# GpSimd in written order, the turning tables in two pieces, a tile's matrices in three

## The chip, the cores and the metric

The kernel runs on one core of a Trainium2 chip. The metric is device time in microseconds (us) of one execution, as the median of several runs. The engines are called by their names in the profile: PE is TensorE, DVE VectorE, ACT ScalarE, POOL GpSimd, SP SyncE (which here only issues DMAs).

## What is computed

One inference step of a decoder trunk: one S5 state-space layer and then one stick-breaking attention layer, over a prompt of 1024 tokens and eight samples of eight new tokens, with a model width of 1024. All of the change lies in the S5 layer:

```python
h = _rms_norm(x, g_pre)
uz = h @ w_in                                  # u and z, 1024 wide each
u, z = uz[..., :SSM_WIDTH], uz[..., SSM_WIDTH:]
...
lam_re, lam_im = mag * cos(dt * a_im), mag * sin(dt * a_im)
bu = w * (b @ u)                               # per group of 16 channels, 64 complex states
h[t] = lam * h[t - 1] + bu[t]                  # complex, over time
y = c_re @ h_re - c_im @ h_im + d_skip * u
...
y = gelu(y); y = y * sigmoid(y @ w_glu + b_glu); y = y * silu(z)
x = x + _rms_norm(y @ w_out, g_post)
```

(The middle lines are shortened from the reference's `_s5_scan`.) The attention layer behind it is the same before and after.

## The kernel before, in words

The time axis is cut in 128 chunks of L = 8 steps, and the eight samples are eight more columns, so that a row of a group is W = 136 columns wide. The 64 groups of 16 channels are worked through as eight tiles `ft` of eight groups; a tile's groups are done in three units of 3, 3 and 2 groups (`ACH`), j = 0, 1, 2. Beside the S5 work TensorE computes u and z themselves, x times w_in, as a stream of chunks called `fills` (`gemm`, L268): a chunk is 24 matmuls (three per 128 rows of x, since values are split in a high and a low part), and three chunks make 128 columns of u or z. A weight tile is split by `weights` (L217) and `split_w` (L138): a copy on ScalarE, and a subtraction on VectorE, or on GpSimd where z is odd.

For a tile `matrices(ft)` (L323) makes what the recurrence needs:

- On VectorE `wb`, and `ep` out of it by two products (`ep`, `tm`) and a subtraction, 1024 wide; eight transposes of `ep` on TensorE (L347), four at a time into one PSUM bank of the pool `m`, which has one buffer; each four are evicted by ScalarE to `et` (L348). VectorE also forms `fk` with `tn` (L351 to 353).
- After a `yield`, eight small matmuls K (L361) into the same bank, four evictions to `kp` (L369), `dk` on GpSimd and its addition on VectorE (L372), and eight DMAs that spread `kp` into `tg`.
- The turning tables: cosine and sine by products of short ones, two halves of three operations each into `cs` with the scratch tile `m`, on GpSimd (VectorE for tile 0), and four DMAs `cf<-cs` (L392) that copy them to all partitions. `cs` and `m` have one buffer, `cf` two.
- Eight DMAs `ug` that load the tile's u in another layout.

`states(ft, j)` (L402) is a unit: S matmuls (L409) into `psb`; two ScalarE copies to `tb` (L416, L417); VectorE multiplies `psb` by the cosine (`psb<-psb,cf`), GpSimd `tb` by the sine (`tb<-tb,cf`), VectorE adds (`psb<-psb,tb`), two or three scans (L424); and the same turning back: two copies to `ts` (L429, L430), `ts<-ts,cf` on GpSimd, `psb<-psb,cf` and the sum `hs` (L434) on VectorE. `outputs` (L438) follows two units later (`ULAG`): the O matmuls (L451, L452), the gelu to `gt` and the stores to `y_d`. All of the helper's `tensor_tensor` carry the line L207.

`manual_schedule` for PE keeps TensorE in the order of the text. The other engines' orders are set by a scheduler that plans by priorities, `OFA` being that of `states`, `outputs` and `matrices`. The main loop (L463 to L484) gives one unit per turn: `states`, a chunk, `outputs`, and in units 1 and 2 the next step of `matrices(ft + 1)`; in the first three tiles one more chunk. Behind the loop y is read back and split into `yh` and `yl` (L496 to L500), while the remaining chunks of z run, and the gate's GEMM (`whi_g`) follows.

Of the kernel before, what the change touches and what calls it, by code (L numbers as in the profile page):

```python
# [10 lines left out]
F32 = mybir.dt.float32  # L11
# [4 lines left out]
ALU = mybir.AluOpType  # L16
# [9 lines left out]
NC = SEQ // L  # L26
# [7 lines left out]
KT = 8  # L34
# [23 lines left out]
K_UBC, K_UBS, K_UAC, K_UAS, K_U = 0, 16, 32, 40, 48  # L58


def bc(ap, axis, n):
    shape = list(ap.shape)
    a = ap.unsqueeze(axis)
    shape.insert(axis, n)
    return a.to_broadcast(shape)
# [6 lines left out]
def rstd(nc, pool, ss, out, n, mul, tag, eng=None):  # L72

    E = eng or nc.vector
    v = pool.tile([128, n], F32, name=f"v_{tag}", tag="rs_v")
# [62 lines left out]
def split_w(nc, pool, raw, tag, shape, eng=None, bufs=2):  # L138

    hi = pool.tile(shape, F32R, name=f"whi_{tag}", tag="whi", bufs=bufs)  # L140
    lo = pool.tile(shape, F32R, name=f"wlo_{tag}", tag="wlo", bufs=bufs)
    nc.scalar.activation(hi, raw, AF.Copy)
    (eng or nc.vector).tensor_tensor(lo, raw, hi, op=ALU.subtract)
    return hi, lo
# [58 lines left out]
def s5_layer(tc, nc, io, wp, bank, cst, gains, ident, sgn, zs_d, u_d, y_d, s2):  # L203
    V, Q = nc.vector, nc.gpsimd

    def tt(eng, o, a, b, op):
        eng.tensor_tensor(o, a, b, op=op)  # L207

    with ExitStack() as sx:
        rows = sx.enter_context(tc.tile_pool(name="a_row", bufs=2, side="right"))  # L210
        big = sx.enter_context(tc.tile_pool(name="a_x", bufs=1, side="right"))
        st = sx.enter_context(ExitStack())
# [4 lines left out]
        def weights(which, ft):  # L217

            with tc.high_priority(2 * OFA):
                wraw = wp.tile([128, KT, 128], F32, name=f"wraw_{which}{ft}", tag="wraw", bufs=1)  # L220

                (nc.scalar if which == "u" else nc.sync).dma_start(wraw, io["a_win"][ft + (KT if which == "z" else 0)])
                return split_w(nc, wp, wraw, f"{which}{ft}", [128, KT, 128], Q if which == "z" and ft % 2 else V)


        gpre = start.tile([128, D], F32, name="gpre")
# [4 lines left out]
        for t in (8, 0, 1, 2, 3, 4, 5, 6, 7):  # L231
# [14 lines left out]
            for i in range(2):  # L246
# [6 lines left out]
                for c, (t0, m) in enumerate(ACH):  # L253
                    if t < 8:
                        if not t0 <= t < t0 + m:
                            continue
                        src, oh, ol = p3, xh[c][:, ks, t - t0, 0:NC], xl[c][:, ks, t - t0, 0:NC]
                        nc.scalar.activation(oh, src, AF.Copy)
                        tt(V, ol, src, oh, ALU.subtract)
                    else:  # L260
                        p4 = p3.rearrange("p a (s t) -> p a t s", t=TS)
                        src, oh, ol = p4[:, :, t0 : t0 + m], xh[c][:, ks, :, NC:W], xl[c][:, ks, :, NC:W]
                        nc.scalar.activation(oh, src, AF.Copy)
                        tt(V, ol, src, oh, ALU.subtract)
            if t == 0:
                w_first = weights("u", 0)
# [19 lines left out]
        def fill(n):  # L286
            for _ in range(n):
                next(fills, None)
# [7 lines left out]
        uu = par.tile([128, G // 2, K_U], F32, name="uu")  # L296
# [10 lines left out]
        tp = st.enter_context(tc.tile_pool(name="a_t", bufs=1, reuse_waits="tile"))  # L307
# [12 lines left out]
        sst = par.tile([128, G, NS], F32, name="sst")  # L320
        made, rows_in, rows_out, started = {}, {}, {}, {}

        def matrices(ft):  # L323

            gs = slice(ft * 8, ft * 8 + 8)
            pk = pk_all[:, gs, :]
            sb = tp.tile([128, 4, 8, GC], F32, name=f"sb{ft}", tag="sb", bufs=2)
            nc.scalar.dma_start(sb, io["s5_bc"][ft, :, 0:4])
            wb = tp.tile([128, 4, 8, GC], F32, name=f"wb{ft}", tag="wb")
            tt(V, wb[:, 0:2], sb[:, 0:2], bc(bc(wri[:, 0, gs], 2, GC), 1, 2), ALU.mult)  # L330
            tt(V, wb[:, 2:4], sb[:, 0:2][:, ::-1], bc(wri[:, 1:3, gs], 3, GC), ALU.mult)
            tt(V, wb[:, 0:2], wb[:, 0:2], wb[:, 2:4], ALU.add)
            V.tensor_scalar(sb[:, 2:4], sb[:, 2:4], sgn, None, op0=ALU.mult)

            ep = tp.tile([128, 8, L, GC], F32, name=f"ep{ft}", tag="ep")
            tm = tp.tile([128, 8, L, GC], F32, name=f"tm{ft}", tag="tm")
            lrv = pk[:, :, K_LR : K_LR + 8][:, :, ::-1]
            liv = pk[:, :, K_LI : K_LI + 8][:, :, ::-1]
            tt(V, ep, bc(lrv, 3, GC), bc(wb[:, 0], 2, L), ALU.mult)
            tt(V, tm, bc(liv, 3, GC), bc(wb[:, 1], 2, L), ALU.mult)  # L340
            tt(V, ep, ep, tm, ALU.subtract)
            et = tp.tile([128, 8, 128], F32, name=f"et{ft}", tag="et", bufs=2)
            for i in range(2):
                ps = bank("m")
                for j in range(4):
                    g = 4 * i + j
                    nc.tensor.transpose(ps[:, j * 128 : (j + 1) * 128], ep[:, g].rearrange("p a b -> p (a b)"), ident)  # L347
                nc.scalar.activation(et[:, 4 * i : 4 * i + 4, :], ps.rearrange("p (a b) -> p a b", a=4), AF.Copy)  # L348
            fk = tp.tile([128, 8, L + 1, GC], F32, name=f"fk{ft}", tag="fk", bufs=2)
            tm2 = tp.tile([128, 8, L + 1, GC], F32, name=f"tn{ft}", tag="tm")  # L350
            tt(V, fk, bc(pk[:, :, K_LR : K_LR + 9], 3, GC), bc(sb[:, 2], 2, L + 1), ALU.mult)  # L351
            tt(V, tm2, bc(pk[:, :, K_LI : K_LI + 9], 3, GC), bc(sb[:, 3], 2, L + 1), ALU.mult)
            tt(V, fk, fk, tm2, ALU.subtract)
            tg = tgs[ft % 2]
            yield
            kp = tp.tile([16, 8, 128], F32, name=f"kp{ft}", tag="kp")
            ps = bank("m")
            for i in range(2):
                for j in range(4):
                    g = 4 * i + j  # L360
                    nc.tensor.matmul(  # L361
                        ps[32 * j : 32 * j + 16, i * 128 : (i + 1) * 128],
                        wb[:, 0, g, :],
                        fk[:, g, 0:L, :].rearrange("p a b -> p (a b)"),
                        start=True,
                        stop=True,
                    )
            for j in range(4):
                nc.scalar.activation(kp[:, j::4, :], ps[32 * j : 32 * j + 16, 0:256].rearrange("p (a b) -> p a b", a=2), AF.Copy)  # L369
            dk = tp.tile([16, 8, GC], F32, name=f"dk{ft}", tag="dk")  # L370
            tt(Q, dk, bc(ident[:16, 0:16], 1, 8), bc(dcol[:, gs], 2, GC), ALU.mult)
            tt(V, kp[:, :, 0:GC], kp[:, :, 0:GC], dk, ALU.add)  # L372
            for t in range(L):
                nc.sync.dma_start(tg[t * GC : (t + 1) * GC, :, GC * t : 128], kp[:, :, 0 : 128 - GC * t])
            ph = uu[:, ft * 4 : ft * 4 + 4, :]
            cs = tp.tile([128, 2, 4, 8, 16], F32, name=f"cs{ft}", tag="cs")
            m = tp.tile([128, 4, 8, 16], F32, name=f"m{ft}", tag="m")
            uac, uas = (bc(ph[:, :, b : b + 8], 3, 16) for b in (K_UAC, K_UAS))
            ubc, ubs = (bc(ph[:, :, b : b + 16], 2, 8) for b in (K_UBC, K_UBS))
            E = Q if ft else V  # L380
            tt(E, cs[:, 0], uac, ubc, ALU.mult)
            tt(E, m, uas, ubs, ALU.mult)
            tt(E, cs[:, 0], cs[:, 0], m, ALU.subtract)
            tt(E, cs[:, 1], uas, ubc, ALU.mult)
            tt(E, m, uac, ubs, ALU.mult)
            tt(E, cs[:, 1], cs[:, 1], m, ALU.add)
            cof = tp.tile([128, 2, 8, NC], F32, name=f"cf{ft}", tag="cf", bufs=2)
            for i in range(2):
                src = cs[64 * i : 64 * i + 64].rearrange("p e g a b -> p e (g a b)")
                for h in range(2):  # L390
                    dst = cof[64 * h : 64 * h + 64, :, 4 * i : 4 * i + 4, :].rearrange("p e g c -> p e (g c)")
                    nc.sync.dma_start(dst, src)  # L392
            made[ft] = pk, et, fk, tg, cof[:, 0], cof[:, 1]

            ug = work.tile([128, 8, W], F32, name=f"ug{ft}", tag="ug")
            usrc = u_d[ft].rearrange("(g c) (t n) -> t c g n", c=GC, t=L)
            for t in range(L):
                nc.sync.dma_start(ug[t * GC : (t + 1) * GC], usrc[t])
            rows_in[ft] = ug
            yield  # L400
# [58 lines left out]
        def ahead(gen):  # L459
            with tc.high_priority(OFA):  # L460
                next(gen)

        first = matrices(0)  # L463
        fill(7)
        ahead(first)
        fill(1)
        ahead(first)
        nxt = None
        for n in range(3 * KT + ULAG):
            ft, j = divmod(n, 3)  # L470
            if n < 3 * KT:
                with tc.high_priority(OFA):
                    states(ft, j)
            if j == 1 and ft + 1 < KT:
                nxt = matrices(ft + 1)
            fill(1)
            if n >= ULAG:
                with tc.high_priority(OFA):
                    outputs(*divmod(n - ULAG, 3))
            if nxt and j:  # L480
                if j == 2 and ft < 3:
                    fill(1)
                ahead(nxt)
                nxt = nxt if j == 1 else None  # L484
# [958 lines left out]
```

## Time and profile before

| | |
|---|---|
| median of 3 runs | 1510.89 us (1508.28 to 1511.17) |
| profiled execution | 1508.97 us, its span 1507.2 us |
| mean granted clock of TensorE in the span | 0.982 |
| busy in the span: PE, DVE, ACT, POOL | 1417.8, 925.2, 716.4, 491.0 us |
| S5 layer | about the first 345 us of the span |

Times in the rows are in us from the start of the span, durations marked as means in groups are ns. A timeline row is: start, duration, engine, line, operation, what is written and read, the shape, and in brackets the engine's idle time before it and what ended it. A wait of several causes is named by the one that came last.

### The profile page before, as it was taken

How to read it: one execution, taken by the hardware profiler on the slowest of the kernel's cores; microseconds unless marked ns; L12 is line 12 of the kernel's file. 1: busy time of each engine (PE TensorE's matmuls, PEld its weight loads, DVE VectorE, ACT ScalarE, POOL GpSimd, SP SyncE). 2: the span in 40 equal slices, each digit the busy share in tenths (PEclk: the TensorE clock that was granted, in tenths of full speed). 3: DMA queues.
4: the chain of work that ended last, by engine and by line, in shares of the span. 5: the costliest groups of instructions: out<-in, count | busy, mean ns of one | idle time of the engine just before them, and what ended most of it. 6: DMA issues, size and time to landing. Idle time of an engine off the chain costs nothing.

```text
span 1507.2 us, 26829 instructions
## 1 busy us (share of the span) xinstructions
PE 1417.8 (94%) x9648; PEld 1150.1 (76%) x9648; DVE 925.2 (61%) x1507; ACT 716.4 (48%) x1424; POOL 491.0 (33%) x473
## 2 busy tenths in 40 slices
PE   4979878899999989999999999999998999998997
PEld 4979877899977879999988877666565665564766
DVE  6977887746754541010122149997888888789545
ACT  5324444544434533232333346675665657576321
POOL 6555656323421123222211012433323233334300
PEclk9998999999999999999999999999999999999999
DMA  5444555473223353232288764979877786754026
GB/s 196 114 139 115 151 146 137 129 252 135 71 92 120 112 203 116 84 114 87 87 311 295 257 233 159 352 268 332 294 277 273 263 288 231 260 201 140 11 80 214
DMA packets 129670, 276.41 MB, mean 183 GB/s; under 512 B 21633, under 2 KB 66562, under 8 KB 129538
## 3 DMA queue, kind: packets, MB, share of 16 engines
q1 hardware_dynamic: 127234, 268.41, 53.1%
q10 hardware_dynamic: 2304, 6.29, 1.3%
q8 instruction: 76, 1.25, 0.3%
q14 instruction: 56, 0.46, 0.1%
HBM read 224.55 MB, written 39.35 MB: 175 GB/s over the span
## 4 chain that ended last, share of the span: by engine, by line
PE 73%; DVE 6%; DMA 4%; issue 2%; POOL 2%; ACT 2%; SPq 1%; DVEq 0%; POOLq 0%; ACTq 0%
PE psmm L149 6%; PE psmm L151 6%; PE psmm L150 6%; PE psqk L150 6%; PE psqk L149 6%; PE psqk L151 6%; PE psa L992 5%; PE psb L1225 5%; PE psa L1033 4%; PE psb L1207 4%; PE psqk L1182 3%; PE psqk L1183 2%; PE psa L149 2%; PE psa L151 2%; PE psa L150 2%
## 5 line engine op out<-in xcount | busy, mean ns | idle before, releaser
L1163 POOL TENSOR_TENSOR ql<-q,qh 128x256 fp32r<-128x256 f32 x64 | 64.7, 1011 | 284.7 <-ACT qh L1162 240.1
L1184 ACT ACTIVATE F<-psqk,bp 128x384 f32<-128x384 f32 (+2 forms) x192 | 111.2, 579 | 63.6 <-PE psqk L1183 48.8
L1189 DVE TENSOR_TENSOR_SCAN F<-F,maskb 128x256 f32<-128x256 f32 (+3 forms) x128 | 130.8, 1027 | 16.0 <-ACT F L1184 15.5
L1192 POOL TENSOR_TENSOR S<-S,F 128x255 f32<-128x255 f32 (+3 forms) x64 | 100.5, 1571 | 115.3 <-DVE F L1191 28.5
L1185 ACT ACTIVATE S<-psqk,bp 128x384 f32<-128x384 f32 (+2 forms) x192 | 111.3, 582 | 22.5 <-PE psb L1207 22.5
L1207 PE MATMUL psb<-cst,S 128*128 128x128 f32 x576 | 96.8, 285 | 4.9 <-DVE og L1229 3.8
L1207 PEld LDWEIGHTS psb<-cst,S 128*128 128x128 f32 x576 | 67.1, 143 | 35.6 <-issue 20.5
L1191 DVE TENSOR_TENSOR_SCAN F<-F 128x384 f32<-128x384 f32 (+1 forms) x64 | 78.6, 1228 | 20.4 <-ACT F L1184 19.8
L1225 PE MATMUL psb<-at,vr 128*64 128x256 f32 (+1 forms) x640 | 90.0, 369 | 0.7 <-DVE at L1211 0.7
L992 PE MATMUL psa<-vp,sat 128*32 128x256 f32 x1024 | 86.0, 388 | 0.0
L1182 PE MATMUL psqk<-ks,qh 128*128 128x384 f32 (+2 forms) x192 | 77.6, 404 | 7.1 <-DVE ks L1147 5.4
L1033 PE MATMUL psa<-kp,qbd 128*32 128x256 f32 x1024 | 75.5, 389 | 0.4 <-PE psb L1207 0.4
L1225 PEld LDWEIGHTS psb<-at,vr 128*64 128x64 f32 x640 | 46.7, 137 | 36.1 <-issue 10.5
L1211 DVE TENSOR_TENSOR at<-psb,maskb 128x384 f32<-128x384 f32 (+3 forms) x128 | 60.2, 478 | 20.7 <-PE psb L1207 20.2
L149 PE MATMUL psmm<-x,whi_g 128*128 128x408 f32 (+1 forms) x192 | 66.6, 347 | 1.1 <-DVE gt L782 1.1
L149 PE MATMUL psmm<-xh,whi_u 128*128 128x408 f32 (+1 forms) x192 | 66.6, 347 | 0.2 <-ACT zt L277 0.2
L149 PE MATMUL psmm<-xh,whi_z 128*128 128x408 f32 (+1 forms) x192 | 66.7, 347 | 0.0
L986 DVE TENSOR_TENSOR_SCAN sF<-sF 128x513 f32<-128x513 f32 x32 | 44.4, 1388 | 36.1 <-ACT sF L983 35.8
L1182 PEld LDWEIGHTS psqk<-ks,qh 128*128 128x128 f32 x192 | 37.2, 194 | 38.1 <-ACT S L1185 13.0
L150 PE MATMUL psmm<-xl,whi_u 128*128 128x408 f32 (+1 forms) x192 | 65.4, 341 | 0.1
L1183 PE MATMUL psqk<-ks,ql 128*128 128x384 f32 (+2 forms) x192 | 65.5, 343 | 0.0
L150 PE MATMUL psmm<-x,whi_g 128*128 128x408 f32 (+1 forms) x192 | 65.1, 339 | 0.0
(452 smaller groups left out, 4224.4 us busy)
## 6 DMA issues: line engine op xcount, KB each, us to landing
kp<-cache_kT SPq DMA_DIRECT2D x128, 512.0 KB, 6.0
vp<-cache_v SPq DMA_DIRECT2D x128, 512.0 KB, 5.7
cf<-cs SPq DMA_DIRECT2D x32, 256.0 KB, 4.2
q<-q_d SPq DMA_DIRECT2D x128, 64.0 KB, 4.6
u_d<-ut SPq DMA_DIRECT2D x8, 544.0 KB, 2.9
ug<-u_d SPq DMA_DIRECT2D x64, 68.0 KB, 2.7
zs_d<-zt SPq DMA_DIRECT2D x8, 544.0 KB, 4.4
y_d<-gt SPq DMA_DIRECT2D x64, 68.0 KB, 2.3
```

What stands on the lines that cost most here:

```text
L149: nc.tensor.matmul(ps, sh, mh, start=(k == 0), stop=False)
L150: nc.tensor.matmul(ps, sh, ml, start=False, stop=False)
L151: nc.tensor.matmul(ps, sl, mh, start=False, stop=(k == n - 1))
L992: self.nc.tensor.matmul(po[32 * r : 32 * r + 32, 0:256], a[:, 32 * r : 32 * r + 32], rhs[:, r * 256 : (r + 1) * 256], start=start, stop=stop)
L1033: nc.tensor.matmul(ps[32 * r : 32 * r + 32, half * 256 : half * 256 + 256], self.qbd[:, 2 * r + e, s, :], kt[:, :, 2 * r + e, :], start=(e ...
L1182: nc.tensor.matmul(ps[:, :m], qh[:, w], ks[:, c0 : c0 + m], start=True, stop=False)
L1184: nc.scalar.activation(F[:, c0 : c0 + m], ps[:, :m], AF.Sigmoid, bias=bp[:, 1, h : h + 1], scale=-0.125)
L1185: nc.scalar.activation(S[:, c0 : c0 + m], ps[:, :m], AF.Sigmoid, bias=bp[:, 0, h : h + 1], scale=0.125)
L1189: V.tensor_tensor_scan(fr, fr, self.maskb[:, 512 - m : 512][:, ::-1], 1.0, ALU.mult, ALU.max)
L1192: (Q if i % 2 else V).tensor_tensor(S[:, 0 : n - 1], S[:, 0 : n - 1], F[:, 1:n], op=ALU.mult)
L1207: nc.tensor.transpose(ps[:, j * 128 : (j + 1) * 128], S[:, (j0 + j) * 128 : (j0 + j + 1) * 128], self.ident)
L1225: nc.tensor.matmul(po[hs, o:256], self.vr[pi][:, j, hs], ats[hh][j // 4][:, j % 4, o:256], start=(j == 0), stop=(j == nj - 1))
```

## The change

It has four parts. The subtraction of every z split runs on VectorE. `manual_schedule` holds GpSimd too, from the start of the loop's set-up: its instructions stand in the order of the text. The turning tables leave `matrices` for a generator `tables(ft)` with two steps, which the loop calls for the tile ahead, in units 0 and 1, right behind `states`; the four DMAs come with the second step. `matrices` yields once more, between its first and its second four transposes, so that it has three pieces, taken in unit 1, in unit 2 behind `states`, and at the end of unit 2. At the start one chunk more stands ahead of tile 0's first unit, six and three single ones, in place of seven and one.

```diff
-                return split_w(nc, wp, wraw, f"{which}{ft}", [128, KT, 128], Q if which == "z" and ft % 2 else V)
+                return split_w(nc, wp, wraw, f"{which}{ft}", [128, KT, 128])
...
+        st.enter_context(tc.manual_schedule(engines={mybir.EngineType.PE, mybir.EngineType.Pool}))
+        turns = {}
+        def tables(ft):
...
+            E = Q if ft else V
+            tt(E, cs[:, 0], uac, ubc, ALU.mult)
+            tt(E, m, uas, ubs, ALU.mult)
+            tt(E, cs[:, 0], cs[:, 0], m, ALU.subtract)
+            yield
+            cof = tp.tile([128, 2, 8, NC], F32, name=f"cf{ft}", tag="cf", bufs=2)
+            tt(E, cs[:, 1], uas, ubc, ALU.mult)
+            tt(E, m, uac, ubs, ALU.mult)
+            tt(E, cs[:, 1], cs[:, 1], m, ALU.add)
...
+                    nc.sync.dma_start(dst, src)
+            turns[ft] = cof
+            yield
...
             for i in range(2):
+                if i:
+                    yield
                 ps = bank("m")
...
-        first = matrices(0)
-        fill(7)
-        ahead(first)
-        fill(1)
-        ahead(first)
+        nxt = tables(0)
+        ahead(nxt)
+        ahead(nxt)
+        first = matrices(0)
+        fill(6)
+        for _ in range(3):
+            fill(1)
+            ahead(first)
         nxt = None
         for n in range(3 * KT + ULAG):
             ft, j = divmod(n, 3)
+            if j == 1 and ft + 1 < KT:
+                nxt = matrices(ft + 1)
             if n < 3 * KT:
                 with tc.high_priority(OFA):
                     states(ft, j)
-            if j == 1 and ft + 1 < KT:
-                nxt = matrices(ft + 1)
+            if j == 0 and ft + 1 < KT:
+                turn = tables(ft + 1)
+            if j < 2 and ft + 1 < KT:
+                ahead(turn)
+            if nxt and j == 2:
+                ahead(nxt)
             fill(1)
```

How this moves the instructions is seen at three places. The first is GpSimd in tile 1. `tb` and `ts` are the turnings of the units (0, 3, 6 is the unit's first group), `cs` and `m` the tables, `dk` the small product of `matrices`. Before:

```order
L207 TENSOR_TENSOR tb_0_1377<-tb_0_1377,cf_1359 128x384
L207 TENSOR_TENSOR dk_1631<-cst,dcol 16x128
L207 TENSOR_TENSOR cs_1926<-uu 128x512 x2
L207 TENSOR_TENSOR cs_1926<-cs_1926,m_1927 128x512
L207 TENSOR_TENSOR m_1927<-uu 128x512
L207 TENSOR_TENSOR cs_1926<-cs_1926,m_1927 128x512
L207 TENSOR_TENSOR m_2185<-uu 128x512
L207 TENSOR_TENSOR ts_0_1387<-ts_0_1387,cf_1359 128x384
L207 TENSOR_TENSOR tb_3_1440<-tb_3_1440,cf_1359 128x384
L207 TENSOR_TENSOR ts_3_1450<-ts_3_1450,cf_1359 128x384
L207 TENSOR_TENSOR tb_6_1531<-tb_6_1531,cf_1359 128x256
L207 TENSOR_TENSOR ts_6_1540<-ts_6_1540,cf_1359 128x256
```

and with the change:

```order
L207 TENSOR_TENSOR tb_0_1412<-tb_0_1412,cf_1221 128x384
L207 TENSOR_TENSOR ts_0_1422<-ts_0_1422,cf_1221 128x384
L207 TENSOR_TENSOR cs_1430<-uu 128x512
L207 TENSOR_TENSOR m_1431<-uu 128x512
L207 TENSOR_TENSOR cs_1430<-cs_1430,m_1431 128x512
L207 TENSOR_TENSOR tb_3_1473<-tb_3_1473,cf_1221 128x384
L207 TENSOR_TENSOR ts_3_1483<-ts_3_1483,cf_1221 128x384
L207 TENSOR_TENSOR cs_1430<-uu 128x512
L207 TENSOR_TENSOR m_1431<-uu 128x512
L207 TENSOR_TENSOR cs_1430<-cs_1430,m_1431 128x512
L207 TENSOR_TENSOR tb_6_1562<-tb_6_1562,cf_1221 128x256
L207 TENSOR_TENSOR ts_6_1571<-ts_6_1571,cf_1221 128x256
```

Before, the table of tile 3 (`cs_1926`) stood between `tb` and `ts` of unit 0, with the first product of tile 4's (`m_2185`) behind it. Now tile 2's table stands there, a half behind `ts` of each of the units 0 and 1 and ahead of the next `tb`.

The second place is TensorE in tile 3, at the transposes for tile 4 (`psm<-cst,ep`), behind the O matmuls (`psa`) and around unit 2's S matmuls (`psb`). Before:

```order
L451 MATMUL psa_2060<-ug_1655,tg_796 128x136
L452 MATMUL psa_2060<-hs_794,fk_1523 128x136
L347 MATMUL psm_2087<-cst,ep_2081 128x128 x4
L347 MATMUL psm_2093<-cst,ep_2081 128x128 x4
L409 MATMUL psb_2104<-ug_1939,et_1795 128x136 x2
```

and with the change:

```order
L464 MATMUL psa_2101<-ug_1683,tg_796 128x136
L465 MATMUL psa_2101<-hs_794,fk_1585 128x136
L378 MATMUL psm_2128<-cst,ep_2122 128x128 x4
L422 MATMUL psb_2134<-ug_1968,et_1843 128x136 x2
L378 MATMUL psm_2154<-cst,ep_2122 128x128 x4
```

The S matmuls now stand between the two lots of transposes, where before these stood together.

The third place is VectorE in tile 2, around the forming of `ep` for tile 4. L437 is the line of the scans, `wlo` a weight split, `hs` and `l` a unit's results. Before:

```order
L207 TENSOR_TENSOR hs_794<-psb_1813,ts_6_1825 128x2x127
L207 TENSOR_TENSOR l_800<-psb_1813,ts_6_1825 128x2
L207 TENSOR_TENSOR wb_2076<-sb_2074,wri 128x256 x2
L207 TENSOR_TENSOR wb_2076<-wb_2076 128x256
L207 TENSOR_TENSOR kp_1901<-kp_1901,dk_1915 16x8x16
L207 TENSOR_TENSOR ep_2081<-pk,wb_2076 128x1024
L207 TENSOR_TENSOR tm_2082<-pk,wb_2076 128x1024
L207 TENSOR_TENSOR psb_1948<-psb_1948,cf_1934 128x3x128
L207 TENSOR_TENSOR ep_2081<-ep_2081,tm_2082 128x1024
L207 TENSOR_TENSOR sst<-psb_1948,pk 128x24
L207 TENSOR_TENSOR tn_2100<-pk,sb_2074 128x1152
```

and with the change:

```order
L437 SCALAR_TENSOR_TENSOR psb_1754<-rho,psb_1754 128x128 x2
L207 TENSOR_TENSOR wb_2117<-sb_2115,wri 128x256 x2
L437 SCALAR_TENSOR_TENSOR psb_1754<-rho,psb_1754 128x128
L143 TENSOR_TENSOR wlo_z_2265<-wraw_z_2262,whi_z_2264 128x1024
L207 TENSOR_TENSOR wb_2117<-wb_2117 128x256
L207 TENSOR_TENSOR ep_2122<-pk,wb_2117 128x1024
L207 TENSOR_TENSOR psb_1754<-psb_1754,cf_1491 128x3x128
L207 TENSOR_TENSOR tm_2123<-pk,wb_2117 128x1024
L207 TENSOR_TENSOR psb_1850<-psb_1850,cf_1491 128x2x128
L207 TENSOR_TENSOR hs_792<-psb_1754,ts_3_1768 128x3x127
L207 TENSOR_TENSOR l_800<-psb_1754,ts_3_1768 128x3
L207 TENSOR_TENSOR ep_2122<-ep_2122,tm_2123 128x1024
```

Before, `ep` was formed behind the last results of the tile, at the border to the next. Now it is formed during unit 1, a weight split stands among unit 1's scans, and `ep`'s last step behind unit 1's results.

## Rows read from the trace of the kernel before

**Rows 1.** Windows, 90 to 318 us: PE, PEld, DVE, ACT, POOL busy (instructions); clock; DMA; GB/s

```profile
90.00:318.00 228.00, 192.05 (x1311) 186.06 (x1312) 163.90 (x290) 100.39 (x229) 123.27 (x98) 0.94 0.53 138
```

**Rows 2.** Waits of TensorE, 88 to 318 us: total, times, longest (us)

```profile
PE psm L347 <- ACT et L348: 28.4, 8, 8.0
```

**Rows 3.** Timeline of VectorE: first adds of tiles 0, 6 and 7; the last `hs`

```profile
108.33 0.57 DVE L207 TENSOR_TENSOR psb<-psb,tb 128x384 f32<-128x384 f32 x1 [4.60 <-POOL tb L207]
...
273.08 0.57 DVE L207 TENSOR_TENSOR psb<-psb,tb 128x384 f32<-128x384 f32 x1
...
291.88 0.57 DVE L207 TENSOR_TENSOR psb<-psb,tb 128x384 f32<-128x384 f32 x1
...
306.22 0.42 DVE L207 TENSOR_TENSOR hs<-psb,ts 128x254 f32<-128x254 f32 x1 [0.39 <-POOL ts L207]
```

**Rows 4.** Timeline of ScalarE and TensorE around one eviction, tile 3

```profile
193.51 0.49 ACT L429 ACTIVATE ts<-psb 64x384 f32<-64x384 f32 x1 [4.44 <-POOL cs L207]
...
198.29 0.60 ACT L348 ACTIVATE et<-psm 128x512 f32<-128x512 f32 x1
...
198.94 0.66 PE L347 MATMUL psm<-cst,ep 128*128 128x128 f32 x4 [4.01 <-ACT et L348]
```

**Rows 5.** Waits of GpSimd, 46 to 345 us

```profile
POOL cs L207 <- DMA cf<-cs: 23.6, 7, 6.6
```

**Rows 6.** Groups of GpSimd by line and shape, 90 to 278 us

```profile
L207 POOL TENSOR_TENSOR cs<-cs,m 128x512 f32<-128x512 f32 x14 | 18.9, 1353 | 0.4
L207 POOL TENSOR_TENSOR cs<-uu 128x512 f32<-128x512 f32 x12 | 17.7, 1491 | 18.4 <-DMA cf<-cs 18.4
L207 POOL TENSOR_TENSOR tb<-tb,cf 128x384 f32<-128x384 f32 x14 | 17.0, 1212 | 3.7 <-issue 3.1 <-POOL ts L207 0.3 <-ACT tb L417 0.2
L207 POOL TENSOR_TENSOR m<-uu 128x512 f32<-128x512 f32 x13 | 16.7, 1285 | 0.6
L207 POOL TENSOR_TENSOR dk<-cst,dcol 16x128 f32<-16x128 f32 x7 | 14.3, 2049 | 9.2 <-DVE kp L207 9.2
L207 POOL TENSOR_TENSOR ts<-ts,cf 128x384 f32<-128x384 f32 x13 | 13.0, 1002 | 29.6 <-ACT ts L430 29.5
L143 POOL TENSOR_TENSOR wlo_z<-wraw_z,whi_z 128x1024 fp32r<-128x1024 f32 x3 | 7.9, 2637 | 0.1
```

**Rows 7.** Groups of VectorE by line and shape, 90 to 278 us

```profile
L424 DVE TENSOR_TENSOR_SCAN psb<-rho,psb 128x128 f32<-128x128 f32 x51 | 21.7, 425 | 1.3
L207 DVE TENSOR_TENSOR fk<-fk,tn 128x1152 f32<-128x1152 f32 x7 | 15.5, 2219 | 0.0
...
L207 DVE TENSOR_TENSOR fk<-pk,sb 128x1152 f32<-128x1152 f32 x6 | 10.3, 1712 | 0.6 <-PE psa L452 0.6
...
L143 DVE TENSOR_TENSOR wlo_z<-wraw_z,whi_z 128x1024 fp32r<-128x1024 f32 x2 | 2.4, 1208 | 0.0
```

**Rows 8.** Timelines of VectorE and GpSimd at 211 us; all `dk` (min/median/max ns)

```profile
212.22 1.21 DVE L207 TENSOR_TENSOR tm<-pk,wb 128x1024 f32<-128x1024 f32 x1
...
211.24 2.45 POOL L207 TENSOR_TENSOR dk<-cst,dcol 16x128 f32<-16x128 f32 x1 [2.59 <-DVE kp L207]
...
L207 POOL TENSOR_TENSOR dk<-cst,dcol x8: 392/2452/2764, 71.7 to 260.1; 16x128 f32<-16x128 f32 x8
```

**Rows 9.** Transfers `cf`: issues (ns) and landing; GpSimd's longest wait for one

```profile
L392 SPq DMA_DIRECT2D cf<-cs x32: 597/631/1422, 79.0 to 273.8; - x32
...
DMA to landing us min/median/max: 3.0/4.2/6.5
...
251.04 2.08 POOL L207 TENSOR_TENSOR cs<-uu 128x512 f32<-128x512 f32 x2 [6.62 <-DMA cf<-cs]
```

**Rows 10.** Timeline of TensorE: last GEMM matmuls, last O, first `yl`

```profile
312.75 0.35 PE L150 MATMUL psmm<-xl,whi_z 128*128 128x408 f32 x1
...
313.68 0.39 PE L451 MATMUL psa<-ug,tg 128*128 128x136 f32 x2
...
342.32 0.45 PE L150 MATMUL psmm<-yl,whi_g 128*128 128x408 f32 x1 [1.97 <-DVE yl L500]
```

More of the change, by code (lines that the diff above doesn't have):

```diff
@@ L321, in s5_layer @@
         made, rows_in, rows_out, started = {}, {}, {}, {}
+        st.enter_context(tc.manual_schedule(engines={mybir.EngineType.PE, mybir.EngineType.Pool}))
+        turns = {}
+        def tables(ft):
+            ph = uu[:, ft * 4 : ft * 4 + 4, :]
+            cs = tp.tile([128, 2, 4, 8, 16], F32, name=f"cs{ft}", tag="cs")
+            m = tp.tile([128, 4, 8, 16], F32, name=f"m{ft}", tag="m")
+            uac, uas = (bc(ph[:, :, b : b + 8], 3, 16) for b in (K_UAC, K_UAS))
+            ubc, ubs = (bc(ph[:, :, b : b + 16], 2, 8) for b in (K_UBC, K_UBS))
+            E = Q if ft else V
[7 more added lines that the diff above has]
+            tt(E, cs[:, 1], cs[:, 1], m, ALU.add)
+            for i in range(2):
+                src = cs[64 * i : 64 * i + 64].rearrange("p e g a b -> p e (g a b)")
+                for h in range(2):
+                    dst = cof[64 * h : 64 * h + 64, :, 4 * i : 4 * i + 4, :].rearrange("p e g c -> p e (g c)")
+                    nc.sync.dma_start(dst, src)
+            turns[ft] = cof
+            yield
         def matrices(ft):
@@ L374, in matrices @@
                 nc.sync.dma_start(tg[t * GC : (t + 1) * GC, :, GC * t : 128], kp[:, :, 0 : 128 - GC * t])
[L375 to L393, printed above, removed]
+            made[ft] = pk, et, fk, tg, turns[ft][:, 0], turns[ft][:, 1]
             ug = work.tile([128, 8, W], F32, name=f"ug{ft}", tag="ug")
```

## The prediction

> **What bounds the kernel now.** The change lies in the S5 layer, some 230 of the span's 1507.2 us, so I read that stretch alone. First the busy time by window: between 90 and 318 us TensorE is busy 192.05 of 228.00 us at a mean granted clock of 0.94, VectorE 163.90, GpSimd 123.27, ScalarE 100.39 [rows 1]. No engine is full; some 36 us of TensorE are lost. Next the waits of TensorE: 28.4 us of them stand before the transposes of L347, eight times, 3.6 each, on ScalarE's eviction of the first four matrices [rows 2]. The second four want the one PSUM bank that the first four fill, and follow them directly.
>
> Third, the pace. I take the first add of each tile (`psb<-psb,tb`, VectorE) as a mark. It stands at 108.33 in tile 0, 273.08 in tile 6 and 291.88 in tile 7 [rows 3]: six rounds of 27.46, then one of 18.80, in which no further tile is prepared.
>
> Fourth, why the eviction is late. The timeline at 193 us shows it: ScalarE's copy `ts` waited 4.44 us "for POOL cs" (a buffer that GpSimd had to release, since a table lay ahead of the turning in GpSimd's queue), the eviction came 4.3 us behind it in ScalarE's queue, and TensorE stood 4.01 us [rows 4]. So the loop's own chain (VectorE, ScalarE, GpSimd, by turns) holds TensorE up, by way of queues. In GpSimd's own waits 23.6 us are tables that wait until the transfers have read the table before [rows 5].
>
> **The change part by part.** The sum is made against the profiled execution, 1508.97 us; the median of the three runs, 1510.89, is 1.9 above it and I leave that out. About 0.2%, 3 us, is what a measurement of this kernel can tell from no change.
>
> *The odd z splits.* Four splits of 2.64 us leave GpSimd [rows 6] and cost VectorE 1.21 each [rows 7]. GpSimd has room; what counts is that one weight split, of u or z, now stands among the scans of unit 1 in a tile.
>
> *Transposes in two pieces.* TensorE's order is T, S, T for T, T, S. Between the two T stand two or three S matmuls, under 1 us of TensorE, whereas the bank comes free when ScalarE has got to the eviction, and in tiles 3 to 6 that still has the same copies ahead of it. I take at most 1 us of each wait as gone, and count it at nothing, because the next thing TensorE reaches (S, O) waits for the chain below.
>
> *The tables.* Before, GpSimd made them up to two tiles ahead, between turnings. Now each half stands right behind the `ts` turning of unit 0 and of unit 1 and ahead of the next `tb`, and the transfers start only behind the second half; the first turning of the next tile needs them. That makes a loop, whose parts are: add 0.57 [rows 3], three scans of 0.425 = 1.28 [rows 7], two ScalarE copies of 0.49 = 0.98 [rows 4], GpSimd `ts` 1.00, half a table 1.49 + 1.29 + 1.35 = 4.13, `tb` of unit 1 1.21 [rows 6], together 9.17; then unit 1's add, scans, copies, `ts` and half table without a new `tb`, 7.96; then the transfers, an issue of 0.63 and a landing of 4.2 [rows 9], 4.83, and `tb` 1.21. Sum 23.17. Eleven handovers from engine to engine at 0.1 (the one from the end of the eviction to the transposes took 0.05 [rows 4]; 0.1 is an estimate) make 24.3, and the split among the scans 25.5.
>
> Two things move that. VectorE and GpSimd hold each other up: `dk`, 0.39 us at its shortest, took 2.45 beside `tm` and the `ep` before it, and ended 0.26 after `tm` [rows 8]. The change brings VectorE's run of `ep` and `tm`, for the tile after next, forward into units 1 and 2, where the half tables run. I price one meeting at `dk`'s mean less its shortest, 2.05 - 0.39 = 1.66 [rows 6, 8], and take 1.5 meetings in a round: 2.5. That makes **28.0 a round**. Bounds: each table operation alone on the engine at its shortest, no split and no meeting, about 22 to 24; at the other end VectorE's pair `fk`, 1.71 + 2.22 [rows 7], which the change puts between add and scans in tiles 1 and 2, a landing as late as 6.5 [rows 9] and a meeting at every half, 31 to 33. Beside the landing runs unit 2 (`tb`, add, scans, copies, `ts`, then `dk`), about 4.7 us with the shortest `dk`, 6.4 with its mean; so the two are close, and the latter would add 1.5.
>
> A wait that goes: before, a table waited as much as 6.62 us for the transfers of the one before [rows 9]. Now these have long landed, since the turning of unit 0 stands ahead and needed them. It is paid once instead of hidden two tiles ahead.
>
> The Trainium skill, page "SBUF — State Buffer", section "Who interferes with whom", says that a VectorE instruction with two inputs in SBUF contends with a GpSimd instruction that reads SBUF, by an exclusive lock: who issues first holds it, and the other is fully blocked. Our `dk`, blocked until `tm` had ended, agrees. By that rule in its full form every half table meets a VectorE run, which is the third rival below.
>
> *SyncE.* The four `cf` transfers stand behind eight `y_d` and eight `ug` in text order. Issues cost 0.6 and these wait for nothing that is later than the table, so nothing; a late `u_d` store ahead of them would add its wait to the round.
>
> *Start.* One more chunk of the GEMM, 24 matmuls, stands before the first S. Five matmuls take 0.93 us (312.75 to 313.68) [rows 10], so a chunk takes 4.5. But the first add had waited 4.60 for GpSimd's `tb` [rows 3], which the tables of later tiles held up and no longer do. So +0.5, with bounds of -4 and +4.5.
>
> *Rounds.* Six at 28.0 against 27.46: +3.2. The seventh has no tile behind it to prepare, so no meetings, but its table is still made in the loop: 25.5 against 18.80, +6.7.
>
> *End.* Before, the last add to the last O (which ends about 1.1 after 313.68) took 22.9, though the last `hs` came at 306.22, 14.3 after the add [rows 3, 10]: TensorE was behind. Now TensorE has been waiting in each round and has a chunk at most in hand, so 14.3 + most of 4.5 = 18: -4.9.
>
> *Tail.* Behind the last O four chunks of z instead of five cover the way of y through memory to `yl`, which TensorE already waited 1.97 us for [rows 10]. Cover lost is up to 4.5, but that chunk was spent at the start and gate chunks move up: I take +2.5, bounds 0 and 4.5.
>
> Sum: 0.5 + 3.2 + 6.7 - 4.9 + 2.5 = +8.0; 1508.97 + 8.0 = **1517.0**.
>
> With x for a round, and the last 2.5 shorter, the total is 7x - 188.0 over the profiled time, so the sign hangs on x: below 26.7 it is faster by over 0.2%, above 27.55 slower, against the median of the runs.
>
> **The rivals.**
>
> *The loop is shorter than I make it (faster).* The half tables fall into the time in which GpSimd would only wait, and the meetings do not happen. Then x is 25.5 without a meeting, 1502, or 24.5 when the split is hidden too, 1495; the floor is TensorE, 192.05/228.00 of 27.46 = 23.1 of work in a round [rows 1]. For it: GpSimd is idle for 105 of 228 us, and its two-tile lead bought nothing that the rows show, only waits [rows 4, 5]. Against it: a transfer's landing enters the loop. It decides when the six rounds average under 26.7. Chance 0.31.
>
> *VectorE's queue sets the pace as before.* VectorE works 163.90 of 228.00, 19.7 a round, in long runs that the scans stand behind; if it is what every round waits for, where GpSimd does its tables matters little: rounds stay, the last too, and only start and tail move, 0.5 + 0 to 2.5: 1510 to 1512. Chance 0.17.
>
> *Two meetings in each round.* Both halves held up by a full run: 25.5 + 2 x 1.66 = 28.8, sum 12.8, 1522. Chance 0.08.
>
> *Much slower.* `fk` in the loop in two rounds and most operations of GpSimd at double length: 31.5, the last 28.5, sum 32, 1541. For it: the mean of `dk`, five times its shortest [rows 6, 8]. Chance 0.10.
>
> That the change does not do what it says is partly in my case: the second transposes may wait behind the eviction as before. It costs nothing where the loop paces.
>
> **How the numbers follow.** My case has 0.34, slower by 6 on the median. Slower by over 0.2%: 0.34 + 0.08 + 0.10 = 0.52. Faster: 0.31. Within 0.2%: 0.17. The range goes from the lower end of the first rival to the upper bounds of my case (x = 30.7, the landing or unit 2 late): 1496 to 1536; it leaves out the fastest of the first rival, about 0.06, and the last rival, 0.10. My case's own range is 1514 to 1524.
>
> **What would show it.** Right: first adds 28 us apart in tiles 1 to 6 and 25 in the last; GpSimd's `tb` of unit 0 waiting on the transfers of `cf` by name; ScalarE's copies waiting for scans rather than for tables; table operations over 2 us beside `ep` and `tm`; TensorE's waits moved from L347 to S and O, with their sum no smaller. Wrong: rounds under 26.7 with TensorE busy over 0.87 of the window, or unit 0's `tb` released by ScalarE's copies, the transfers long landed; then the tables are no loop. Rounds like those of before with VectorE's own queue as last releaser would be the second rival.

## The result, and the profile after

The changed kernel takes **1521.06 us**, the median of four runs (1520.42 to 1522.92), against 1510.66 us of the kernel before: 10.4 us more by the medians. The ratio is given as 1.0076, with a 95% interval of 1.0061 to 1.0091, so it is slower by some 9 to 14 us; 1517.0 was forecast, in a range of 1496 to 1536. The profiled execution's span grew from 1507.2 to 1519.8 us, by 12.6.

The window 90 to 318 us of the changed kernel, with the columns of [rows 1]:

```profile
90.00:318.00 228.00, 181.76 (x1197) 175.45 (x1198) 159.82 (x281) 95.43 (x216) 112.67 (x94) 0.90 0.50 126
```

Every engine is less busy than in [rows 1], and TensorE's granted clock fell from 0.94 to 0.90: all of them wait more. So what paces the stretch is no engine's work. TensorE's waits, 88 to 330 us:

```profile
PE psb L422 <- DMA u_d<-ut: 13.6, 2, 7.2
PE psa L465 <- DVE hs L207: 11.4, 5, 3.7
PE psm L378 <- ACT et L379: 8.9, 5, 4.1
PE psb L422 <- DMA zs_d<-zt: 7.0, 1, 7.0
...
PE psb L422 <- DMA ug<-u_d: 2.9, 1, 2.9
```

The 28.4 us before the transposes [rows 2] are 8.9 now. That the pieces alone did this is not shown: in the runs below the wait is 17.7 with only the z splits moved, and 14.8 with the pieces but the scheduler's order on GpSimd. But O now waits 11.4 for `hs`, and S 23.5 for transfers on SyncE's queue. (S needs the loads `ug`; two of these three rows name a store that stands in the same queue.) The first adds on VectorE, as in [rows 3]:

```profile
106.78 0.56 DVE L207 TENSOR_TENSOR psb<-psb,tb 128x384 f32<-128x384 f32 x1
...
286.69 0.57 DVE L207 TENSOR_TENSOR psb<-psb,tb 128x384 f32<-128x384 f32 x1
...
310.97 0.57 DVE L207 TENSOR_TENSOR psb<-psb,tb 128x384 f32<-128x384 f32 x1
```

That is 29.98 a round for six rounds and 24.28 for the last, against 27.46 and 18.80. The last O, as in [rows 10]:

```profile
334.78 0.39 PE L464 MATMUL psa<-ug,tg 128*128 128x136 f32 x2
```

With these marks the 12.6 us are split up in full:

| step | before | after | difference | forecast |
|---|---|---|---|---|
| start to first add | 108.33 | 106.78 | -1.6 | +0.5 |
| six rounds | 164.75 | 179.91 | +15.2 | +3.2 |
| last round | 18.80 | 24.28 | +5.5 | +6.7 |
| last add to last O | 21.80 | 23.81 | +2.0 | -4.9 |
| last O to the end of the span | 1193.5 | 1185.0 | -8.5 | +2.5 |

Inside a round GpSimd shows the two speeds of a table. Its timeline in tile 2, first half and second half:

```profile
173.57 1.06 POOL L207 TENSOR_TENSOR cs<-uu 128x512 f32<-128x512 f32 x1
174.59 1.05 POOL L207 TENSOR_TENSOR m<-uu 128x512 f32<-128x512 f32 x1
175.72 1.27 POOL L207 TENSOR_TENSOR cs<-cs,m 128x512 f32<-128x512 f32 x1
176.96 1.01 POOL L207 TENSOR_TENSOR tb<-tb,cf 128x384 f32<-128x384 f32 x1
...
185.27 2.04 POOL L207 TENSOR_TENSOR cs<-uu 128x512 f32<-128x512 f32 x1
187.27 2.04 POOL L207 TENSOR_TENSOR m<-uu 128x512 f32<-128x512 f32 x1
189.39 2.28 POOL L207 TENSOR_TENSOR cs<-cs,m 128x512 f32<-128x512 f32 x1
191.64 0.74 POOL L207 TENSOR_TENSOR tb<-tb,cf 128x256 f32<-128x256 f32 x1
```

and VectorE beside the second half:

```profile
184.82 1.57 DVE L207 TENSOR_TENSOR tm<-pk,wb 128x1024 f32<-128x1024 f32 x1
...
187.18 1.22 DVE L207 TENSOR_TENSOR ep<-ep,tm 128x1024 f32<-128x1024 f32 x1
...
188.43 2.09 DVE L207 TENSOR_TENSOR tn<-pk,sb 128x1152 f32<-128x1152 f32 x1
```

The same operations take 1.05 alone and 2.04 beside VectorE's run; the half table took 3.4 and then 6.4 us. The `tb` behind each half starts without a gap, and so it is in tiles 0 to 6: these turnings wait for the tables and for nothing else.

Where else the round grew is seen on VectorE. The start of tile 2, between the first add and the scans (L437):

```profile
166.41 0.57 DVE L207 TENSOR_TENSOR psb<-psb,tb 128x384 f32<-128x384 f32 x1
167.71 1.36 DVE L207 TENSOR_TENSOR fk<-pk,sb 128x1152 f32<-128x1152 f32 x1 [0.73 <-PE psa L465]
168.98 0.42 DVE L437 TENSOR_TENSOR_SCAN psb<-rho,psb 128x128 f32<-128x128 f32 x1
169.31 1.34 DVE L207 TENSOR_TENSOR fk<-fk,tn 128x1152 f32<-128x1152 f32 x1
170.57 0.88 DVE L437 TENSOR_TENSOR_SCAN psb<-rho,psb 128x128 f32<-128x128 f32 x2
```

Here `ts` on GpSimd starts 6.2 us after the add, in tile 1 6.5, and in tiles 3 to 6, where `fk` comes later, 3.1. And unit 2 of tile 4, of which VectorE's rows are

```profile
250.01 0.42 DVE L207 TENSOR_TENSOR psb<-psb,tb 128x256 f32<-128x256 f32 x1
250.35 1.22 DVE L207 TENSOR_TENSOR ep<-ep,tm 128x1024 f32<-128x1024 f32 x1
251.48 0.42 DVE L437 TENSOR_TENSOR_SCAN psb<-rho,psb 128x128 f32<-128x128 f32 x1
251.81 1.34 DVE L207 TENSOR_TENSOR tn<-pk,sb 128x1152 f32<-128x1152 f32 x1
253.07 0.41 DVE L437 TENSOR_TENSOR_SCAN psb<-rho,psb 128x128 f32<-128x128 f32 x1
```

and GpSimd's

```profile
254.71 0.74 POOL L207 TENSOR_TENSOR ts<-ts,cf 128x256 f32<-128x256 f32 x1 [7.29 <-ACT ts L443]
255.41 0.39 POOL L207 TENSOR_TENSOR dk<-cst,dcol 16x128 f32<-16x128 f32 x1
255.77 0.99 POOL L207 TENSOR_TENSOR tb<-tb,cf 128x384 f32<-128x384 f32 x1
```

GpSimd stood 7.29 us for unit 2's `ts`, because `ep` and `tm` (from 247.74 on) stand ahead of the add and `ep` and `tn` among the scans, and the next tile's `tb` is queued behind it. From the end of the second half to that `tb` it took 9.2 here, 8.5 and 9.8 in tiles 0 and 1, and 4.7 to 5.0 in tiles 2, 3, 5 and 6.

### The profile page after: what moved, and what is told of

It is laid out like the page before. It is cut to its first block, busy times and chain, and to the rows that moved or that the text cites. A ratio compares the mean times of both kernels' runs of the same rounds, so it can differ in the third digit from the quotient of the medians.

```text
span 1519.8 us, 26840 instructions
## 1 busy us (share of the span) xinstructions
PE 1421.0 (94%) x9648; PEld 1155.0 (76%) x9648; DVE 931.5 (61%) x1511; ACT 717.6 (47%) x1424; POOL 477.3 (31%) x469
## 4 chain that ended last, share of the span: by engine, by line
PE 77%; DVE 11%; DMA 3%; POOL 3%; ACT 2%; issue 2%; SPq 2%; DVEq 0%; ACTq 0%; POOLq 0%
PE psmm L149 8%; PE psmm L150 8%; PE psmm L151 8%; PE psqk L149 6%; PE psqk L150 6%; PE psqk L151 6%; PE psa L1015 5%; PE psb L1248 4%; PE psa L1056 4%; PE psb L1230 4%; PE psqk L1205 3%; PE psa L149 2%; PE psqk L1206 2%; PE psa L151 2%; PE psa L150 2%
## 5 line engine op out<-in xcount | busy, mean ns | idle before, releaser
L1186 POOL TENSOR_TENSOR ql<-q,qh 128x256 fp32r<-128x256 f32 x64 | 61.1, 956 | 284.6 <-ACT qh L1185 242.8
L151 PE MATMUL psmm<-x,wlo_g 128*128 128x408 f32 (+1 forms) x192 | 65.5, 341 | 0.2 <-DVE wlo_g L143 0.2
```

The source lines that it names most:

```text
L151: nc.tensor.matmul(ps, sl, mh, start=False, stop=(k == n - 1))
```

## The experiments

The **loop theory**: each round is paced by a chain through GpSimd's queue, in which the half tables stand since the change. Its rival, the **queue theory**: TensorE's new waits for `ug`, which come from SyncE's queue, set the pace. All ratios are against runs of the kernel before on the same chip.

### Undoing GpSimd's written order, and the z splits alone

```diff
-        st.enter_context(tc.manual_schedule(engines={mybir.EngineType.PE, mybir.EngineType.Pool}))
```

> The change without its second part: the scheduler sets GpSimd's order again, and makes tables up to two tiles ahead as in the kernel before; z splits on VectorE and three pieces stay. Loop theory: rounds of 25 to 28, total 1495 to 1512. Queue theory: TensorE's order is the changed one, so near 1521.

1508.83 us, ratio 0.9985 (0.9974 to 0.9996). This one line takes back the whole loss and a little more: it is worth 12 us, and the other parts of the change together are a gain of some 2 us over the kernel before. Rounds were 27.8 and the last 20.5. It has the lowest median of all kernels here that compute the whole layer, but nothing that can be told from the next ones (1508.91 and 1509.62, below).

The line does not act on GpSimd alone. VectorE's order is the scheduler's, and in this run it is another one too. In tile 2, for example, whose first add is at 166.07 here:

```profile
166.66 1.35 DVE L437 TENSOR_TENSOR_SCAN psb<-rho,psb 128x128 f32<-128x128 f32 x3
...
169.60 2.37 DVE L207 TENSOR_TENSOR fk<-pk,sb 128x1152 f32<-128x1152 f32 x1
```

`fk` follows the scans, where in the changed kernel it stands ahead of them. How the 12 us are shared between the two engines' orders is not shown. Between the first adds of tiles 0 and 7 VectorE keeps the changed kernel's order in two of the runs below, the one without the transfers and the one with the loads alone moved, and in no other.

The kernel before with the first part alone:

```diff
-                return split_w(nc, wp, wraw, f"{which}{ft}", [128, KT, 128], Q if which == "z" and ft % 2 else V)
+                return split_w(nc, wp, wraw, f"{which}{ft}", [128, KT, 128])
```

> The kernel before with the z splits on VectorE and nothing else. My price was nothing: 1508 to 1513. If GpSimd's splits were what held ScalarE's evictions in the kernel before (one of them released a copy that had waited 11 us), it is faster by 3 to 8.

1509.62 us, ratio 0.9990 (0.9973 to 1.0007): no difference that can be told. TensorE's wait at the transposes fell from 28.4 to 17.7 us and the six rounds from 27.5 to 26.6 in its profile; little of that is seen in the median. The profiled execution was one of the shortest of the ten, 1504.41 us, 5 below their median.

### Taking the tables out

```diff
-            if j < 2 and ft + 1 < KT:
-                ahead(turn)
+            if j == 1 and ft + 1 < KT:
+                turns[ft + 1] = turns[0]
```

> Leaves out the turning tables of tiles 1 to 7 and their transfers; all tiles use tile 0's, so the outputs are others. Loop theory: a round loses two half tables (3.4 to 6.3 each) and the wait for the transfers, until TensorE's own work of about 23 a round or VectorE's queue is next: rounds 23 to 25, total 1475 to 1495. Queue theory: rounds 28 to 30, total 1510 to 1521.

1491.47 us, ratio 0.9881 (0.9860 to 0.9903): 30 us below the changed kernel, with six rounds of 24.5. The tables and their transfers hold the pace (VectorE's order, which is another here as well, has a share that is not known).

### Taking out only the transfers

Every half table is formed as in the changed kernel; the four DMAs are left out for tiles 1 to 7.

```diff
+            if ft:
+                turns[ft] = turns[0]
+                yield
+                return
             for i in range(2):
                 src = cs[64 * i : 64 * i + 64].rearrange("p e g a b -> p e (g a b)")
```

> Leaves out the transfers of the turning tables of tiles 1 to 7; GpSimd still forms every half table in the same place, and all tiles are turned by tile 0's, so the outputs are others. If the landing is what ends a round (4.83 of it, as the prediction's sum has it), a round falls by 3 to 5: total 1486 to 1500. If unit 2's own way runs beside it and ends with it (the changed kernel's first turnings waited 0.9 at most for a transfer), a round falls by 0 to 1: 1513 to 1521. The queue theory, too, expects a gain, of the 3.2 us that four issues take on SyncE a tile: 1500 to 1510.

1519.52 us, ratio 1.0057 (1.0035 to 1.0080), rounds 29.45: half a microsecond less a round, and a time that cannot be told from the changed kernel's. So the 30 us are not the transfers; they are the forming of the tables on GpSimd, with what VectorE's other order in that run gave. The landing runs beside unit 2 and ends with it. In the changed kernel's waits of GpSimd:

```profile
POOL tb L207 <- DMA cf<-cs: 2.9, 4, 0.9
```

and in this one the row is gone, with the pace the same. SyncE's 28 saved issues changed neither the time nor the waits of S for its transfers (24.5 us, 23.5 in the changed kernel), so on the queue theory this run says little.

### Moving the loads of u

```diff
+            ug = work.tile([128, 8, W], F32, name=f"ug{ft}", tag="ug")
+            ...
             for i in range(2):
                 if i:
                     yield
                 ps = bank("m")
```

> The changed kernel with one thing moved: the eight loads `ug` of the next tile are issued with the first piece of `matrices` instead of the last, so ahead of the `tg` transfers of that tile on SyncE. TensorE waited about 24 us in five S for them. Table theory: rounds stay at 29 to 30, since GpSimd's loop ends them, 1515 to 1522. Queue theory: the three waits of 7 us go, rounds 26 to 28, 1500 to 1508.

1522.94 us, ratio 1.0082 (1.0057 to 1.0108), rounds 29.7. The move did not do what it was meant to do: S still waits 9.3, 7.9 and 6.7 us for transfers, in sum 23.9 against 23.5, so the time alone cannot decide between the theories. The trace of the changed kernel can. In tile 6, where S had waited 6.42:

```profile
276.86 1.70 PE L422 MATMUL psb<-ug,et 128*128 128x136 f32 x6 [6.42 <-DMA u_d<-ut]
```

and ScalarE's first copy of its result:

```profile
283.58 0.49 ACT L429 ACTIVATE tb<-psb 64x384 f32<-64x384 f32 x1
```

S ended at 278.56, 5.0 us before ScalarE came to it, behind unit 2's copies `ts`. In tile 4 it was 4.8 us, and in tile 7, the closest, 0.5. So TensorE's waits for `ug` do not set the pace of the changed kernel, though in the last round they are near it. With GpSimd left to the scheduler (both edits, this one and the one that undoes the written order) the same move:

> Scheduler's order on GpSimd, with the loads `ug` moved as well. Against the same without the move (1508.8): faster by 3 to 10 if the loads bound its rounds, else within 3.

1508.91 us, ratio 0.9986 (0.9971 to 1.0001): no difference to 1508.83. Here too the move left the waits for `ug` standing, 17.1 us against 12.9 without it.

### VectorE's large operations with one input

```diff
-            tt(V, ep, bc(lrv, 3, GC), bc(wb[:, 0], 2, L), ALU.mult)
+            V.tensor_scalar(ep, bc(wb[:, 0], 2, L), 0.5, None, op0=ALU.mult)
```

(and so for `tm`, `fk`, `tn` and the two subtractions, in tiles 1 to 7).

> The changed kernel, GpSimd's order untouched. For tiles 1 to 7 the six large VectorE operations of `matrices` (`ep`, `tm`, `fk`, `tn`) are replaced by a multiplication with a constant that reads one tile in place of two; the turning by the right transition is left out, so the outputs are others. If GpSimd's table operations take 2.0 to 2.3 in place of 1.05 because VectorE reads two inputs beside them, all of them come down to 1.05 to 1.3, a round loses 2 to 3 there and more where those operations stood among scans: rounds 24 to 27, 1488 to 1506. If they are slow for another reason (the transfers, ScalarE), they stay at 2 and rounds at 28 to 30: 1510 to 1521.

The time did not fall, and lies outside both ranges: 1522.54 us, ratio 1.0089 (1.0069 to 1.0109). Yet the first rounds are shorter: 26.3, 28.2, 26.2 and 25.9, where the changed kernel has 28.6, 31.0, 31.3 and 29.5. The groups of GpSimd in this run, 90 to 300 us:

```profile
L207 POOL TENSOR_TENSOR cs<-cs,m 128x512 f32<-128x512 f32 x14 | 20.5, 1461 | 1.1
L207 POOL TENSOR_TENSOR cs<-uu 128x512 f32<-128x512 f32 x14 | 16.6, 1185 | 0.0
```

and in the changed kernel:

```profile
L207 POOL TENSOR_TENSOR cs<-cs,m 128x512 f32<-128x512 f32 x13 | 23.8, 1831 | 1.0
...
L207 POOL TENSOR_TENSOR cs<-uu 128x512 f32<-128x512 f32 x13 | 18.0, 1388 | 0.0
```

(`m<-uu` went from 1472 to 1106; `dk` was at 391 already and is 457 here.) Of the 42 table operations 16 took 2 us or more in the changed kernel and one here, beside a weight split, which still reads two tiles. So VectorE's large operations are what doubled them. That it is the second input is not shown: with one input they are also shorter, 0.69 to 0.74 us in place of 1.22 to 1.35, and they still hold GpSimd up and are held up by it. In tile 6 VectorE and GpSimd have

```profile
285.50 1.18 DVE L388 TENSOR_SCALAR fk<-sb 128x1152 f32<-128x1152 f32 x1
...
286.03 1.57 POOL L207 TENSOR_TENSOR cs<-uu 128x512 f32<-128x512 f32 x1
```

VectorE's order is another, too, with `fk` behind the scans, so the 3.5 us a round are not GpSimd's shorter tables alone. Then the rounds turn to 30.6, 31.2 and 37.1. TensorE's waits say why:

```profile
PE psb L432 <- DMA ug<-u_d: 36.1, 3, 14.6
```

Three S waits of 12 us, and here S does hold the round: the last one ends at 308.39, and ScalarE's copy of it starts at 308.48. In these last rounds the loads take the pace: the queue theory was wrong of the changed kernel and is right of this one.

### The half tables where GpSimd waits

The half table is put between `tb` and `ts` of its unit, where GpSimd stands idle for scans and copies.

```diff
             tt(Q, tb[:, :n], tb[:, :n], sif[:, gl], ALU.mult)
+            if mid:
+                next(mid)
...
```

> Only the place of each half table changes: ahead of `ts` of its unit instead of behind it, so in the time in which GpSimd waits for scans and copies (3.1 to 7 us in the changed kernel). Loop theory (GpSimd's written order makes tables part of the chain from one tile's first add to the next): most of 2 x 3.4 us a round leaves the chain, rounds 24 to 26 in place of 30.0, total 1485 to 1500. Queue theory (TensorE's waits of up to 7 us for the tile's loads behind SyncE's queue set the pace): rounds stay at 29 to 30, total 1515 to 1523.

A miss, above both ranges: 1540.92, ratio 1.0209 (1.0183 to 1.0235). Units did become quicker (in tile 6 the third add came 15.1 us after the first, in the changed kernel 18.8), but S of the next tile then waited:

```profile
PE psb L422 <- DMA ug<-u_d: 62.1, 6, 15.5
```

With the loads moved to the first piece as well, by the same edit as above:

> Both moves: half tables ahead of `ts`, and the loads `ug` with the first piece. If the first move failed because another loop, through SyncE's queue and the loads, took the pace (TensorE waited 62 us in six S for `ug`), this has neither: rounds 24 to 26, 1482 to 1500. If tables ahead of `ts` are bad in themselves, 1530 to 1541 as without the second move.

1527.28 us, ratio 1.0110 (1.0081 to 1.0138); a part only, 48.4 us of these waits are left. The chain of waits of this run shows what S waits for, from the second half table of tile 5 to the S of tile 6 (start, us, what):

```profile
260.98 1.28 POOL cs L207
...
262.28 0.65 SPq L347
...
265.65 1.08 SPq L472
...
275.09 3.71 DMA ug<-u_d
...
279.00 1.02 PE psb L422 x3
```

On SyncE the `cf` transfers (L347), then `y_d` (L472) stand ahead of the loads, so S of tile 6 waits for the table of tile 6, which waits for a turning of tile 5. The table left one chain and joined another through a queue that the scheduler still orders. Two ways round SyncE were tried. The loads on ScalarE's queue:

```diff
-                nc.sync.dma_start(ug[t * GC : (t + 1) * GC], usrc[t])
+                nc.scalar.dma_start(ug[t * GC : (t + 1) * GC], usrc[t])
```

> Half tables ahead of `ts`, the loads `ug` in the first piece and issued on ScalarE's queue, where no transfer of a table stands ahead of them. The two moves before failed, by the trace, because S waited for `ug` behind `cf` on SyncE, 48 us in six waits. With that loop cut, rounds 24 to 27, 1482 to 1505; if tables ahead of `ts` hold the loop up by themselves, 1520 or more.

1533.25 us, ratio 1.0158 (1.0139 to 1.0178). S waits for no load now; instead

```profile
PE psm L383 <- ACT et L384: 55.0, 7, 12.9
```

the eviction of the transposes comes late. In ScalarE's order it stands behind the next unit's copies, with issues of loads between them: in tile 3 the first of these copies waited 5.97 us for scans, until 221.72, and the eviction came at 223.64. And the transfers issued by GpSimd itself, with the loads on SyncE:

```diff
-                    nc.sync.dma_start(dst, src)
+                    (nc.gpsimd if ft else nc.sync).dma_start(dst, src)
```

> As the second of the two earlier moves together (half tables ahead of `ts`, `ug` with the first piece on SyncE), and the transfers `cf` of tiles 1 to 7 are issued by GpSimd itself, behind the second half table. Then nothing on SyncE waits for a table, and the wait of S for `ug` (48 us in six) should go to under 15. If that loop was all that held the move back: rounds 24 to 27, 1482 to 1505. If issuing on GpSimd costs it much, or VectorE's `fk` and the wait of `wb` for K are next, 1505 to 1520. If the half tables are wrong ahead of `ts`, 1525 or more.

1521.24 us, ratio 1.0061 (1.0039 to 1.0082), the best of this family and no better than the changed kernel. An issue on GpSimd took 0.59, and S still waited 37.4 us for `ug` in five times. SyncE's own longest waits in this run, 90 to 330 us, are those of `tg`:

```profile
SPq L410 <- DVE kp L207: 58.5, 7, 15.4
```

The `tg` transfers (L410) stand ahead of the loads on SyncE and wait for `kp`, which VectorE forms. So the loads wait behind VectorE's queue now instead of behind the tables. What cutting that too would give was not run; this branch stays open.

## Why the prediction was right, and where not

The sign, the likeliest case and the range held: slower, by GpSimd's written order, with rounds above 27.55. That the total came so near is luck, and the sign in part too. With the measured round of 29.98 the formula 7x - 188.0 gives 1531; with the forecast round of 28.0 and the measured start, end and tail the sum is 1510.8, no change. Point by point:

- *Pace.* Right: taking the tables out gave 30 us, the scheduler's order 12, with VectorE's order in both. Rounds were 29.98 where I said 28.0, and 24.28 where I said 25.5. As forecast, GpSimd's table operations took over 2 us beside `ep` and `tm`, ScalarE's copies waited for scans and no more for tables, and TensorE's waits moved from the transposes to S and O (in sum 47 us against 37).
- *The landing as a term* (4.83 in the sum of 28.0). Wrong as the thing that ends a round: without it the round shrank by 0.5. The sign that I had named, `tb` of unit 0 waiting for `cf`, came in four of seven tiles, with 0.9 us at most. What stood there was what I had put beside it as close, unit 2's own way. It took 4.7 to 5.0 in four rounds and 8.5 to 9.8 in the three where `ep`, `tn` or a weight split lay among its scans; 7.0 on average over the six.
- *`fk` between add and scans.* I named it for tiles 1 and 2 and left it to the bounds and the last rival. It was there, with 6.2 and 6.5 us to GpSimd's `ts` in place of 3.1; in tile 0 it was 4.6, so 1.3 a round on average. With the 2.1 of the arc before, that is 3.4 a round; the table operations and their `ts` came out 1.1 cheaper than my mean with 1.5 meetings, and the other arcs 0.3, which leaves the 2.0 by which 28.0 fell short. So the term that was mis-sized is VectorE's order, not GpSimd's work.
- *The lock.* The Trainium skill's rule (page "SBUF — State Buffer", section "Who interferes with whom") agrees with the changed kernel's trace: in tile 2 the three table operations ended 0.92, 0.91 and 1.15 us after the VectorE instruction beside them, about the 1.05, 1.05 and 1.27 that they take alone. The run with one input does not test it, since its operations are shorter as well. The rival of two full meetings a round, 1522, is near the measured time, but by other terms: in the six rounds five of twelve half tables met a full run, 5.5 to 6.4 us each, two a shorter one, 4.5, and five none, 3.4 to 3.9.
- *Odd z splits and pieces at nothing.* Right within 2 us, 0.9990 and 0.9985 against the kernel before, but the wait before the transposes fell by far more than the 1 us each that I allowed.
- *End, -4.9.* Wrong: +2.0. I let TensorE have "a chunk at most in hand" behind the last add. The order of the text says otherwise: four chunks with their O stand between that add and the last O in both kernels, TensorE was busy all the time from 311 on, and they take what they take.
- *Tail, +2.5.* Wrong, -8.5. The chunk that is done at the start is one chunk less behind the last O, 4.5 us of TensorE that I did not credit while I charged the start; and the wait for `yl`, 1.97 [rows 10], did not grow but vanished. In the kernel before, the last `yl` on VectorE stood beside a product on GpSimd:

```profile
337.99 3.13 POOL L522 TENSOR_TENSOR yv<-yv,zr 128x1088 f32<-128x1088 f32 x1 [13.12 <-DMA zr<-zs_d]
...
338.66 3.61 DVE L500 TENSOR_TENSOR yl<-yr,yh 128x1088 fp32r<-128x1088 f32 x1
```

  The other `yl` took 1.29; this one ended 1.15 after the product, and TensorE's wait with it. After the change that product comes at 362.47, behind all `yl`. Behind the wait TensorE's granted clock was 0.50 for a while, the 1.2 GHz level (columns as in [rows 1]):

```profile
343.40:346.70 3.30, 3.30 (x12) 3.19 (x11) 1.33 (x3) 0.72 (x2) 0.00 (x0) 0.50 0.93 300
```

  Ten matmuls came 0.34 apart there instead of 0.19, which is 1.5 us; the changed kernel has no wait and 1.00 from 334.78 to 366. That makes 8.0 of the 8.5.

The errors of end, tail and rounds offset each other: the total is nearer than its parts.

## What to carry to other kernels

Work that is moved from "ahead, in the gaps" to a fixed place in an in-order queue joins every chain that passes that queue; follow the ring from a mark back to the same mark, on all engines and DMA queues, and price each arc by its slower side. When one ring is cut, the next one can be only a few per cent shorter, as here, and may run through a queue that nobody wrote (here SyncE's, between tables and loads), so look for it before the move, in the order and not in the busy time. Chunks that leave one end of a program are missing at the other: count them on both ends. And where a scheduler orders the other engines, compare their orders before a run is taken to test one thing.

## What the runs showed of the hardware

A GpSimd operation of 1.05 us took 2.04 beside VectorE's products of two SBUF tiles. VectorE pays as well: `tn` beside the table took 2.09, alone 1.34, and `yl` beside GpSimd's product 3.61, alone 1.29. Beside VectorE's shorter operations with one input the same GpSimd operation took up to 1.57. GpSimd issued a 64x2x512 transfer in 0.59 us, as quickly as SyncE in [rows 9].
